# Macaron encoder kernel: second token tiles turned inside the preceding product, eps on VectorE, the last columns in parts, the S5's gated tiles pipelined

## The chip, the cores and the metric

The kernel runs on one core of one Trainium2 chip. The metric is the device time of one execution in microseconds. On the core, TensorE (PE) multiplies, VectorE (DVE), ScalarE (ACT) and GpSimd (POOL) do the elementwise work, and SyncE (SP) issues most of the loads. Each engine executes its own instructions in program order and waits on semaphores for the others.

## The reference

Two layers on a sequence of 256 tokens with 1024 channels, batch 1, fp32. Each layer has three sub-layers, each of which ends in a LayerNorm.

```python
for i in range(DEPTH):                                   # DEPTH = 2
    h = _layernorm(DN_ALPHA * h + 0.5 * _swiglu(h, ffn_w_in[i, 0], ffn_w_out[i, 0]), ln_g[i, 0], ln_b[i, 0])
    mix = _s5_mixer(h, ...) if i % N_MIXERS == 0 else _gmlp_mixer(h, ...)
    h = _layernorm(DN_ALPHA * h + mix, ln_g[i, 1], ln_b[i, 1])
    h = _layernorm(DN_ALPHA * h + 0.5 * _swiglu(h, ffn_w_in[i, 1], ffn_w_out[i, 1]), ln_g[i, 2], ln_b[i, 2])

def _swiglu(x, w_in, w_out):                             # 1024 -> 2 x 2816 -> 1024
    gate, up = jnp.split(x @ w_in, 2, axis=-1)
    return (jax.nn.silu(gate) * up) @ w_out
...
    y = jax.nn.gelu(y)                                   # end of _s5_mixer; y from the scan
    z = y * jax.nn.sigmoid(y @ w_glu + b_glu)
    return z @ w_out
...
    z = jax.nn.gelu(x @ w_in + b_in)                     # start of _gmlp_mixer
    u, v = jnp.split(z, 2, axis=-1)
    v = _layernorm(v, ln_g, ln_b)
```

## The kernel before

**Tiles.** The tokens are two tiles of 128, t = 0 and 1; `h[t]` (128 tokens x 1024 channels) is the running state. A product needs the channels on the partitions, so `make_xt(t)` turns h of a tile: eight PE transposes of 128x128 into two PSUM tiles (`tps`, L187), an ACT cast of each (L192) that gives `xt` hi, and a DVE subtract (L193) that gives `xt` lo. Every fp32 product is made of three (`mm3`: hi by hi, hi by lo, lo by hi; L201, L202, L203, or L208 to L210 for the products that keep the weights in place).

**Weights.** `Stream` ws brings the weights in blocks of 128x2048 in the order of their use: a load by SP into one of three raw buffers, an ACT cast to hi, a DVE subtract to lo, into one of five slots. `ws.tick(n)` splits up to n blocks and issues the loads that have become possible, so where a tick stands in the code sets where the split stands in ACT's and DVE's order (L96, L97).

**Order.** The sub-layers run ffn, s5, ffn, ffn, gmlp, ffn. The code is written in the order that the engines execute (`tc.manual_schedule()`); nothing moves instructions afterwards. An FFN has 11 chunks of 256 hidden columns, and its second product is accumulated chunk by chunk.

**The end of a sub-layer, `close`.** The last products run tile by tile, t = 0 with columns 0 to 511 and 512 to 1023, then t = 1. After each half DVE forms r from h and the PSUM tile (`layernorm_half`, L239) and its statistics (L240), then `layernorm` aggregates them (L247), `rstd_of` makes the reciprocal deviation on POOL in two instructions (eps added, L221; the power -0.5, L222), and `normalize` does r by gamma (L228) and then times rstd plus beta (L231), all in halves of 512. `make_xt(0)` of the next sub-layer stands inside the products of t = 1. In the last sub-layer there is no next one, and each half of h goes out by a DMA, one from SP and one from ACT.

**The start of the next FFN.** Chunks 0 and 1 are made one tile at a time by `step_in(c, t)`, a product of 24 matmuls of 512 (8 slices of k by 3) into the PSUM tile `ips`, then `in_act`: silu on ACT and the gate product on DVE (`sgg`, L358). `step_in(c, 1)` turns the gated tiles of both chunks on PE in its middle (`finish_g`, L348). The order is (0,0), (1,0), `make_xt(1)`, (0,1), (1,1). In the gMLP `step_v` does the same for v (`zps`).

**The end of the S5.** `finish(n)` for eight tiles of 128 channels: DVE makes the gated product (L1164), a cast (DVE for n < 3, L1168; ACT from 3 on, L1170), and a DVE subtract to lo (L1171). z lies in two buffers in turn. Two halves of a weight block's subtract (`rest(1)`, L119) stand after n = 1 and n = 3. The output product of the S5 follows (`close_mixer`).

Of the kernel before, what the change touches and what calls it, by code (L numbers as in the profile page):

```python
# [154 lines left out]
def hybrid(ctx: ExitStack, tc: tile.TileContext, a: dict, out: bass.AP, subs=SUBS):  # L155
# [63 lines left out]
    def rstd_of(mv, eps):  # L219
        rstd = st_p.tile([P, 2], F32, tag="rstd", name="rstd")  # L220
        nc.gpsimd.tensor_scalar(rstd[:, 0:1], mv[:, 1:2], eps, 1.0, op0=ALU.add, op1=ALU.mult)  # L221
        nc.gpsimd.tensor_tensor(rstd[:, 1:2], rstd[:, 0:1], mhalf, op=ALU.pow)  # L222
        return rstd[:, 1:2]
# [51 lines left out]

    def close(li, si, acc, blocks, mm, gb, hscale, eps, last):

        order = [(n, j) for n in range(2) for j in range(len(blocks))]
        for t in range(2):
            for n, j in order:  # L280
                for kt in range(2):
                    mm(j, t, n, kt, acc[t][n])
                    if (t, n, j, kt) == (1, 1, len(blocks) - 2, 0) and not last:
# [12 lines left out]
            if last:
                for n in range(2):
                    s = slice(512 * n, 512 * n + 512)
                    (nc.sync, nc.scalar)[n].dma_start(out=out[0, P * t:P * t + P, s], in_=h[t][:, s])
# [33 lines left out]
    def ffn(ids, li, si, first, last):  # L333
# [146 lines left out]
        close(li, si, acc, [ids["out"][c] for c in range(c0, NCH)], lambda j, t, n, kt, ps: mm_out(c0 + j, t, n, kt, ps),  # L480
# [48 lines left out]
    def gmlp(plan, par, pool, li, si, first, last):  # L529
# [61 lines left out]
        pend = [step_v(0, 0), step_v(1, 0)]  # L591
        make_xt(1)
# [426 lines left out]
    def s5(plan, res, qp, li, si, first, last):  # L1019
# [140 lines left out]
        def finish(n):  # L1160

            x = half(n)
            z = buf["o"][n % 2][:, 0].rearrange("p q k -> p (q k)")
# [7 lines left out]
            V.tensor_tensor(yx(n, 1), z, yx(n, 0).bitcast(F32), op=SUB)  # L1171
# [182 lines left out]
```

## Time and profile before

| | |
|---|---|
| time, median of 3 runs | 971.5 us (970.46 to 971.52) |
| profiled execution | 971.83 us, span 969.7 us, mean granted clock 0.998 |
| PE busy | 944.7 us, 97% of the span |
| DVE busy | 650.9 us, 67% |
| ACT busy | 426.5 us, 44% |
| POOL busy | 162.8 us, 17% |
| PE clock, 40 slices | 9 in every slice |
| moved | 195.10 MB, mean 201 GB/s |

Busy shares are averages over stages with different limits. In timeline rows the first number is the start and the second the time covered, both in us, then the engine, the line, the operation, what it writes and reads, its shape and how many instructions the row joins; in brackets stand the idle time before it and what ended that. Neighbouring instructions of one engine overlap a little, so that a row that joins several is shorter than their sum. A row of waits has the total in us, the number of times, and the longest. A row of windows has busy time and instructions (x) of PE, its weight loads (PEld), DVE, ACT and POOL, then the granted clock, the DMA share and GB/s.

### The profile page before, as it was taken

The page shows a single profiled execution, that of the slowest core. Times are in us where ns is not written, and L with a number is a line of the kernel's source. Part 1 is how long each engine was busy: PE and PEld are TensorE (multiplying, and loading weights), DVE is VectorE, ACT ScalarE, POOL GpSimd, SP SyncE. Part 2 cuts the span into 40 slices and gives each one's busy share as a digit, 9 for nine tenths or more (in the row PEclk, how much of TensorE's full clock was granted, in tenths as well). Part 3 has the DMA queues.
Part 4 walks back from the last instruction along what each step waited for, and adds up shares of the span by engine and source line. Part 5 has one row for each costly group of instructions (what it writes and reads, how often), then busy time and mean ns, then how long its engine had stood idle before and what let it go on. Part 6 is the DMA issues. An engine that isn't in the chain of part 4 may idle for free.

```text
span 969.7 us, 16611 instructions
## 1 busy us (share of the span) xinstructions
PE 944.7 (97%) x6988; PEld 857.9 (88%) x6988; DVE 650.9 (67%) x805; ACT 426.5 (44%) x504; POOL 162.8 (17%) x240
## 2 busy tenths in 40 slices
PE   7999999999999999999999999999999999999996
PEld 5999999978896799999987999999889879999995
DVE  5889998787998774554667636455788866453635
ACT  5465347535342553434433534353445444444430
POOL 1888910011750100000001000000011010000001
PEclk9999999999999999999999999999999999999999
DMA  8887796958646566365547765636357468465521
GB/s 276 219 249 228 237 318 203 315 200 300 208 141 220 174 198 236 132 224 167 185 163 239 255 222 166 225 133 227 121 173 261 130 203 268 138 220 172 184 78 43
DMA packets 133898, 195.10 MB, mean 201 GB/s; under 512 B 7632, under 2 KB 104576, under 8 KB 133824
## 3 DMA queue, kind: packets, MB, share of 16 engines
q1 hardware_dynamic: 129152, 182.61, 56.8%
q0 software_dynamic: 4384, 10.92, 3.9%
q8 instruction: 54, 0.88, 0.4%
q10 hardware_dynamic: 288, 0.52, 0.1%
q14 instruction: 20, 0.16, 0.0%
HBM read 184.07 MB, written 9.96 MB: 200 GB/s over the span
## 4 chain that ended last, share of the span: by engine, by line
PE 68%; DVE 8%; ACT 2%; issue 1%; POOL 1%; DMA 1%; POOLq 0%; DVEq 0%; ACTq 0%
PE ips L210 11%; PE ips L209 11%; PE ips L208 11%; PE acc L201 7%; PE acc L202 7%; PE acc L203 7%; DVE lo L97 3%; PE pps L1080 2%; PE ips L203 1%; ACT hi L96 1%; DVE lo L89 1%; DMA raw<-in_s_w_in 1%; PE ips L201 1%; PE ips L202 1%; PE zps L209 1%
## 5 line engine op out<-in xcount | busy, mean ns | idle before, releaser
L210 PE MATMUL ips<-xt,lo 128*128 128x256 f32 x1184 | 335.2, 283 | 2.2 <-DVE lo L89 2.2
L208 PE MATMUL ips<-xt,hi 128*128 128x256 f32 x1184 | 335.4, 283 | 0.0
L209 PE MATMUL ips<-xt,hi 128*128 128x256 f32 x1184 | 335.0, 283 | 0.0
L89 DVE TENSOR_TENSOR lo<-raw,hi 128x2048 fp32r<-128x2048 f32 x107 | 242.9, 2291 | 8.7 <-ACT hi L88 8.3
L210 PEld LDWEIGHTS ips<-xt,lo 128*128 128x128 f32 x1184 | 227.1, 192 | 2.6 <-DVE lo L89 2.6
L208 PEld LDWEIGHTS ips<-xt,hi 128*128 128x128 f32 x1184 | 227.1, 192 | 1.5
L209 PEld LDWEIGHTS ips<-xt,hi 128*128 128x128 f32 x1184 | 227.1, 192 | 1.4
L88 ACT CAST hi<-raw 128x2048 fp32r<-128x2048 f32 x107 | 203.9, 1909 | 46.4 <-PE acc L203 26.6
L398 DVE TENSOR_TENSOR sgg<-ips,sgg 128x256 f32<-128x256 f32 x74 | 31.1, 420 | 166.1 <-ACT sgg L397 166.0
L201 PE MATMUL acc<-hi,gt 128*128 128x512 f32 x352 | 137.9, 392 | 0.2 <-ACT gt L406 0.2
L202 PE MATMUL acc<-lo,gt 128*128 128x512 f32 x352 | 137.4, 390 | 0.0
L203 PE MATMUL acc<-hi,gt 128*128 128x512 f32 x352 | 137.0, 389 | 0.0
L397 ACT ACTIVATE sgg<-ips 128x256 f32<-128x256 f32 x74 | 28.4, 383 | 216.4 <-PE ips L210 213.5
L221 POOL TENSOR_SCALAR rstd<-mv 128x1 f32<-128x1 f32 x14 | 10.4, 741 | 634.6 <-DVE mv L247 610.8
L97 DVE TENSOR_TENSOR lo<-raw,hi 128x2048 fp32r<-128x2048 f32 (+2 forms) x52 | 89.6, 1754 | 22.7 <-ACT hi L96 22.6
L203 PEld LDWEIGHTS acc<-hi,gt 128*128 128x128 f32 x352 | 66.1, 188 | 14.3 <-DVE gt L407 0.2
L201 PEld LDWEIGHTS acc<-hi,gt 128*128 128x128 f32 x352 | 66.2, 188 | 13.2 <-ACT gt L406 0.6
L202 PEld LDWEIGHTS acc<-lo,gt 128*128 128x128 f32 x352 | 66.3, 188 | 12.2
L96 ACT CAST hi<-raw 128x2048 fp32r<-128x2048 f32 (+2 forms) x52 | 74.5, 1482 | 4.2 <-DMA raw<-in_ffn_w_in 2.5
L407 DVE TENSOR_TENSOR gt<-sgg,gt 128x256 fp32r<-128x256 f32 x74 | 32.4, 438 | 61.8 <-ACT gt L406 61.8
L406 ACT CAST gt<-sgg 128x256 fp32r<-128x256 f32 x74 | 30.1, 406 | 58.2 <-DVE sgg L398 58.2
L201 PE MATMUL ips<-hi,xt 128*128 128x512 f32 x112 | 46.0, 410 | 3.6 <-ACT xt L192 2.3
(229 smaller groups left out, 1222.1 us busy)
## 6 DMA issues: line engine op xcount, KB each, us to landing
raw<-in_ffn_w_in SPq DMA_DIRECT2D x172, 512.0 KB, 5.7
raw<-in_ffn_w_out SPq DMA_DIRECT2D x44, 1024.0 KB, 5.1
raw<-in_g_w_in SPq DMA_DIRECT2D x8, 1024.0 KB, 6.0
rows<-w SPq DMA_DIRECT2D x8, 512.0 KB, 6.3
raw<-in_s_w_in SPq DMA_DIRECT2D x4, 1024.0 KB, 8.4
raw<-in_s_w_glu SPq DMA_DIRECT2D x4, 1024.0 KB, 5.0
w<-rows SPq DMA_DIRECT2D x8, 512.0 KB, 5.8
tc<-tc SPq DMA_DIRECT2D x16, 256.0 KB, 5.5
```

The source lines that it names most:

```text
L88: nc.scalar.copy(hi, raw)
L89: self.unfinished.append(lambda: nc.vector.tensor_tensor(lo, raw, hi.bitcast(F32), op=ALU.subtract))
L96: nc.scalar.copy(hi[:, s], raw[:, s])
L97: eng[p % len(eng)].tensor_tensor(lo[:, s], raw[:, s], hi[:, s].bitcast(F32), op=ALU.subtract)
L201: nc.tensor.matmul(ps, xh, wh, start=start, stop=False)
L202: nc.tensor.matmul(ps, xh, wl, start=False, stop=False)
L203: nc.tensor.matmul(ps, xl, wh, start=False, stop=stop)
L208: nc.tensor.matmul(ps, wh, xh, start=start, stop=False)
L209: nc.tensor.matmul(ps, wh, xl, start=False, stop=False)
L210: nc.tensor.matmul(ps, wl, xh, start=False, stop=stop)
L398: nc.vector.tensor_tensor(g, ps[:, 1], sg, op=ALU.mult)
L407: nc.vector.tensor_tensor(x[:, 1], g, x[:, 0].bitcast(F32), op=ALU.subtract)
```

## The change

It has four parts. (1) `rstd_of` adds eps on DVE; the power stays on POOL. (2) In the last sub-layer `close_last` takes the place of `close`: columns 512 to 1023 of t = 1 are finished as two products 256 wide in PSUM tiles of their own (`ops`), after the partial sum of the earlier chunks has gone into r; the statistics of t = 1 are taken in 256s, and its output leaves in three DMAs (512, 256, 256). (3) `step_in(1, 0)` and `step_v(1, 0)` take `make_xt(1)` into their middle, after five of the eight slices of k; `step_in(0, 0)` and `step_v(0, 0)` split no block, and step (1, 0) splits its block right behind `make_xt(1)`. (4) `finish(n)` returns the subtract, which is issued after `finish(n + 1)`; z lies in four buffers, tiles 3 and 5 subtract on POOL, and the two halves of the weight block's subtract stand after n = 4 and n = 5.

```diff
     def rstd_of(mv, eps):
         rstd = st_p.tile([P, 2], F32, tag="rstd", name="rstd")
-        nc.gpsimd.tensor_scalar(rstd[:, 0:1], mv[:, 1:2], eps, 1.0, op0=ALU.add, op1=ALU.mult)
+        nc.vector.tensor_scalar(rstd[:, 0:1], mv[:, 1:2], eps, 1.0, op0=ALU.add, op1=ALU.mult)
         nc.gpsimd.tensor_tensor(rstd[:, 1:2], rstd[:, 0:1], mhalf, op=ALU.pow)
...
+    def close_last(acc, blocks, mm, gb, hscale, eps):
+        for t in range(2):
+            r = ln_p.tile([P, D], F32, tag="r", name="r", bufs=2)
+            parts = [(0, 512), (512, 512)] if t == 0 else [(0, 512), (512, 256), (768, 256)]
+            step = parts[-1][1]
+            st = st_p.tile([P, D // step, 6], F32, tag="bst", name="bst")
+            if t == 1:
+                s = slice(512, D)
+                nc.vector.scalar_tensor_tensor(r[:, s], in0=h[t][:, s], scalar=hscale, in1=acc[t][1], op0=ALU.mult, op1=ALU.add)
+            for i, (c, w) in enumerate(parts):
+                s, n = slice(c, c + w), c // 512
+                ps = acc[t][n] if w == 512 else mm_p.tile([P, 512], F32, tag="mm", name="ops")[:, 0:w]
+                for j in range(len(blocks)):
+                    for kt in range(2):
+                        mm(j, t, n, kt, ps, (c % 512, w), w < 512 and j == 0 and kt == 0)
...
+                x, scale = (h[t], hscale) if w == 512 else (r, 1.0)
+                nc.vector.scalar_tensor_tensor(r[:, s], in0=x[:, s], scalar=scale, in1=ps, op0=ALU.mult, op1=ALU.add)
+                for x in range(c, c + w, step):
+                    nc.vector.bn_stats(st[:, x // step], r[:, x:x + step])
+            mv = st_p.tile([P, 2], F32, tag="mv", name="mv")
+            nc.vector.bn_aggr(mv, st)
+            rstd, (g, b) = rstd_of(mv, eps), gb
...
+            for i, (c, w) in enumerate(parts):
+                s = slice(c, c + w)
+                nc.vector.scalar_tensor_tensor(h[t][:, s], in0=r[:, s], scalar=rstd, in1=b[:, s], op0=ALU.mult, op1=ALU.add)
+                (nc.sync, nc.scalar)[i % 2].dma_start(out=out[0, P * t:P * t + P, s], in_=h[t][:, s])
...
-        def step_in(c, t):
+        def step_in(c, t, mid=None, split=1):
             ps = mm_p.tile([P, 512], F32, tag="mm", name="ips")
-            in_mm(ids["in"][c], t, ps, range(4))
+            cut = 5 if mid else 4
+            in_mm(ids["in"][c], t, ps, range(cut))
+            if mid:
+                mid()
             if t:
                 finish_g()
-            ws.tick()
-            in_mm(ids["in"][c], t, ps, range(4, KD))
+            ws.tick(split)
+            in_mm(ids["in"][c], t, ps, range(cut, KD))
             in_act(c, t, ps)
             if t == 1:
                 done(ids["in"][c])
-            ws.tick()
+            ws.tick(split)
...
-            step_in(0, 0)
-            step_in(1, 0)
-            make_xt(1)
+            step_in(0, 0, split=0)
+            step_in(1, 0, lambda: make_xt(1))
             step_in(0, 1)
             step_in(1, 1)
...
-        pend = [step_v(0, 0), step_v(1, 0)]
-        make_xt(1)
+        pend = [step_v(0, 0, split=0), step_v(1, 0, lambda: make_xt(1))]
...
         def finish(n):
             x = half(n)
-            z = buf["o"][n % 2][:, 0].rearrange("p q k -> p (q k)")
+            z = buf["o"][n % 2][:, n // 2 % 2].rearrange("p q k -> p (q k)")
...
-            V.tensor_tensor(yx(n, 1), z, yx(n, 0).bitcast(F32), op=SUB)
+            return lambda: (G if n in (3, 5) else V).tensor_tensor(yx(n, 1), z, yx(n, 0).bitcast(F32), op=SUB)
...
+        second = lambda: None
         for n in range(CT):
-            finish(n)
-            if n in (1, 3):
+            x = finish(n)
+            second()
+            second = x
+            if n in (4, 5):
                 rest(1)
+        second()
```

In the listings below a name carries the number of its tile: h0 and h1 are h of the two token tiles, ips the product of a step, tps a transposed tile in PSUM, sgg a gated tile, lo82 and hi82 the weight block with number 82. Each instruction stands with its line in that kernel.

PE where FFN 2 of layer 0 meets FFN 1 of layer 1, before: the end of step (1, 0), the transposes, the start of step (0, 1).

```order
L203 MATMUL ips_5478<-hi81_5415,xt_96 128x512
L187 MATMUL tps_5506<-ident_85,h1_95 128x128 x4
L187 MATMUL tps_5513<-ident_85,h1_95 128x128 x4
L201 MATMUL ips_5520<-hi78_5274,xt_96 128x512
L202 MATMUL ips_5520<-lo78_5275,xt_96 128x512
L203 MATMUL ips_5520<-hi78_5274,xt_96 128x512
```

PE at the same place after:

```order
L201 MATMUL ips_5471<-hi81_5415,xt_96 128x512
L202 MATMUL ips_5471<-lo81_5416,xt_96 128x512
L203 MATMUL ips_5471<-hi81_5415,xt_96 128x512
L187 MATMUL tps_5487<-ident_85,h1_95 128x128 x4
L187 MATMUL tps_5494<-ident_85,h1_95 128x128 x4
L201 MATMUL ips_5471<-hi81_5415,xt_96 128x512
L202 MATMUL ips_5471<-lo81_5416,xt_96 128x512
L203 MATMUL ips_5471<-hi81_5415,xt_96 128x512
```

The transposes of h1 stand nine matmuls of step (1, 0) earlier, and those nine follow them.

DVE at that place, before: the split of blocks 81 and 82, the gate products of chunks 0 and 1, the lo parts of xt.

```order
L97 TENSOR_TENSOR lo81_5416<-raw81_5282,hi81_5415 128x512 x4
L97 TENSOR_TENSOR lo82_5457<-raw82_5295,hi82_5456 128x2048
L358 TENSOR_TENSOR sgg_5475<-ips_5443,sgg_5475 128x256
L358 TENSOR_TENSOR sgg_5503<-ips_5478,sgg_5503 128x256
L193 TENSOR_TENSOR xt_96<-tps_5506,xt_96 128x512
L193 TENSOR_TENSOR xt_96<-tps_5513,xt_96 128x512
L352 TENSOR_TENSOR gt_5536<-tps_5533,gt_5536 128x128
```

DVE there after:

```order
L97 TENSOR_TENSOR lo81_5416<-raw81_5282,hi81_5415 128x512 x4
L392 TENSOR_TENSOR sgg_5468<-ips_5443,sgg_5468 128x256
L193 TENSOR_TENSOR xt_96<-tps_5487,xt_96 128x512
L193 TENSOR_TENSOR xt_96<-tps_5494,xt_96 128x512
L97 TENSOR_TENSOR lo82_5502<-raw82_5295,hi82_5501 128x2048
L392 TENSOR_TENSOR sgg_5517<-ips_5471,sgg_5517 128x256
L386 TENSOR_TENSOR gt_5536<-tps_5533,gt_5536 128x128
```

The subtract of block 82 moved from ahead of the gate products to behind the two of xt, and the gate product of chunk 1 stands behind it. ACT's cast of block 82 moved in the same way, behind its two casts of xt and ahead of the silu of chunk 1.

DVE at the end of the S5, before, the first four of the eight tiles (rot is z or the gate, y the scan's output, lo44 the weight block whose subtract is done in halves):

```order
L1164 SCALAR_TENSOR_TENSOR rot_2668<-rot_2664,y_2517 128x4x64
L1168 CAST xt_96<-rot_2668 128x2x128
L1171 TENSOR_TENSOR xt_96<-rot_2668,xt_96 128x2x128
L1164 SCALAR_TENSOR_TENSOR rot_2669<-rot_2664,y_2517 128x4x64
L1168 CAST xt_96<-rot_2669 128x2x128
L1171 TENSOR_TENSOR xt_96<-rot_2669,xt_96 128x2x128
L119 TENSOR_TENSOR lo44_3490<-raw44_3321,hi44_3489 128x1024
L1164 SCALAR_TENSOR_TENSOR rot_2668<-rot_2665,y_2517 128x4x64
L1168 CAST xt_96<-rot_2668 128x2x128
L1171 TENSOR_TENSOR xt_96<-rot_2668,xt_96 128x2x128
L1164 SCALAR_TENSOR_TENSOR rot_2669<-rot_2665,y_2517 128x4x64
L1171 TENSOR_TENSOR xt_96<-rot_2669,xt_96 128x2x128
```

DVE there after:

```order
L1203 SCALAR_TENSOR_TENSOR rot_2668<-rot_2664,y_2517 128x4x64
L1207 CAST xt_96<-rot_2668 128x2x128
L1203 SCALAR_TENSOR_TENSOR rot_2669<-rot_2664,y_2517 128x4x64
L1207 CAST xt_96<-rot_2669 128x2x128
L1210 TENSOR_TENSOR xt_96<-rot_2668,xt_96 128x2x128
L1203 SCALAR_TENSOR_TENSOR rot_2668<-rot_2665,y_2517 128x4x64
L1207 CAST xt_96<-rot_2668 128x2x128
L1210 TENSOR_TENSOR xt_96<-rot_2669,xt_96 128x2x128
L1203 SCALAR_TENSOR_TENSOR rot_2669<-rot_2665,y_2517 128x4x64
L1210 TENSOR_TENSOR xt_96<-rot_2668,xt_96 128x2x128
L1203 SCALAR_TENSOR_TENSOR rot_2668<-rot_2666,y_2518 128x4x64
L119 TENSOR_TENSOR lo44_3490<-raw44_3321,hi44_3489 128x1024
```

A tile's subtract stands behind the next tile's product (and cast), the subtract of tile 3 is gone from DVE, and the halves of lo44 stand later. On POOL the subtracts of tiles 3 and 5 stand ahead of the DMAs that load gamma and beta of that sub-layer's LayerNorm.

More of the change, by code (lines that the diff above doesn't have):

```diff
@@ L274, in new_acc @@
         return [acc_p.tile([P, 512], F32, tag="acc", name="acc") for _ in range(2)]
+    def close_last(acc, blocks, mm, gb, hscale, eps):
[13 more added lines that the diff above has]
+                        mm(j, t, n, kt, ps, (c % 512, w), w < 512 and j == 0 and kt == 0)
+                    if t == 0 and i == 0 and j < 2:
+                        ws.tick()
+                    if (t, i) == (1, len(parts) - 1):
+                        ws.done(blocks[j])
+                x, scale = (h[t], hscale) if w == 512 else (r, 1.0)
[5 more added lines that the diff above has]
+            rstd, (g, b) = rstd_of(mv, eps), gb
+            for n in range(2):
+                s = slice(512 * n, 512 * n + 512)
+                nc.vector.scalar_tensor_tensor(r[:, s], in0=r[:, s], scalar=mv[:, 0:1], in1=g[:, s], op0=ALU.subtract, op1=ALU.mult)
+            for i, (c, w) in enumerate(parts):
+                s = slice(c, c + w)
+                nc.vector.scalar_tensor_tensor(h[t][:, s], in0=r[:, s], scalar=rstd, in1=b[:, s], op0=ALU.mult, op1=ALU.add)
+                (nc.sync, nc.scalar)[i % 2].dma_start(out=out[0, P * t:P * t + P, s], in_=h[t][:, s])
@@ L276, in close @@
     def close(li, si, acc, blocks, mm, gb, hscale, eps, last):
+        if last:
+            return close_last(acc, blocks, mm, gb, hscale, eps)
         order = [(n, j) for n in range(2) for j in range(len(blocks))]
@@ L282, in close @@
                     mm(j, t, n, kt, acc[t][n])
-                    if (t, n, j, kt) == (1, 1, len(blocks) - 2, 0) and not last:
+                    if (t, n, j, kt) == (1, 1, len(blocks) - 2, 0):
                         make_xt(0, next_kind[li, si] == "s5")
@@ L290, in close @@
                     sums = layernorm_half(t, acc[t][0], 0, hscale)
-            if t == 1 and not last:
+            if t == 1:
                 ws.tick(1)
             layernorm(t, acc[t], gb, hscale, eps, sums)
-            if t == 1 and not last and next_kind[li, si] != "s5":
+            if t == 1 and next_kind[li, si] != "s5":
                 ws.tick(1, 4)
[L296 to L299, printed above, removed]
     def plan_ffn(li, fi, fine):
@@ L439, in start_in, with mm_out @@
             done(ids["in"][0])
-        def mm_out(c, t, n, kt, ps):
+        def mm_out(c, t, n, kt, ps, cols=(0, 512), start=False):
             gh, gl = (gts[c, kt][:, j, P * t:P * t + P] for j in range(2))
             wh, wl = ws.get(ids["out"][c])
-            s = slice(D * kt + 512 * n, D * kt + 512 * n + 512)
-            mm3(ps, gh, gl, wh[:, s], wl[:, s], c == 0 and kt == 0, c == NCH - 1 and kt == 1)
+            s = slice(D * kt + 512 * n + cols[0], D * kt + 512 * n + sum(cols))
+            end = NCH - 4 if last and (t, n) == (1, 1) and cols[1] == 512 else NCH - 1
+            mm3(ps, gh, gl, wh[:, s], wl[:, s], start or c == 0 and kt == 0, c == end and kt == 1)
         def step_out(c, t):
@@ L479, in ffn @@
         c0 = NCH - 3
-        close(li, si, acc, [ids["out"][c] for c in range(c0, NCH)], lambda j, t, n, kt, ps: mm_out(c0 + j, t, n, kt, ps),
+        close(li, si, acc, [ids["out"][c] for c in range(c0, NCH)], lambda j, *args: mm_out(c0 + j, *args),
               gb, 2 * ALPHA, 4 * EPS, last)
```

13 lines of the change are left out of this document (8 added, 5 removed).

## The prediction

> **What bounds the kernel now.** I read first the engine totals (the table ahead), then the list of what TensorE (PE) waited for, then windows between the joints of the sub-layers, then the timeline engine by engine at each place where a wait stood.
>
> ```profile
> PE tps L187 <- DVE h L231: 2.3, 2, 1.5
> PE ips L201 <- ACT xt L192: 2.3, 3, 0.8
> PE acc L201 <- ACT xt L1170: 1.5, 3, 0.5
> 341.00:505.00 164.00, 164.00 (x1132) 153.46 (x1131) 88.28 (x81) 67.48 (x70) 1.69 (x2) 1.00 0.58 193
> ```
>
> Inside an FFN PE never stops: from 341 to 505 it was busy 164.00 of 164.00 us, at a granted clock of 1.00. The number of matmuls is almost the same after the change, so time can only come from the waits. The three waits shown (us in total, times, longest) are 6.1 us, and they stand where the change works: LayerNorm's result (h) before its transposes, the second token tile's operand (xt) at the three entries of an FFN, and the gated tiles at the S5's end; the gMLP's entry is shown below. A wait also costs the interval in which PE starts again, so each loss below is taken from start to start.
>
> **The joints (step_in, step_v).** Here FFN 2 of layer 0 meets FFN 1 of layer 1.
>
> ```profile
> 505.19 1.03 PE L187 MATMUL tps<-ident,h 128*128 128x128 f32 x8
> 506.76 0.39 PE L201 MATMUL acc<-hi,gt 128*128 128x512 f32 x1
> 510.68 1.92 ACT L96 CAST hi<-raw 128x2048 fp32r<-128x2048 f32 x1
> 515.83 4.69 DVE L97 TENSOR_TENSOR lo<-raw,hi 128x512 fp32r<-128x512 f32 x5
> 519.22 1.03 PE L187 MATMUL tps<-ident,h 128*128 128x128 f32 x8
> 519.86 1.07 ACT L192 CAST xt<-tps 128x512 fp32r<-128x512 f32 x2
> 520.44 0.75 DVE L358 TENSOR_TENSOR sgg<-ips,sgg 128x256 f32<-128x256 f32 x2
> 521.11 1.28 DVE L193 TENSOR_TENSOR xt<-tps,xt 128x512 fp32r<-128x512 f32 x2
> 522.18 0.39 PE L201 MATMUL ips<-hi,xt 128*128 128x512 f32 x1
> 524.25 0.60 PE L348 MATMUL tps<-ident,sgg 128*128 128x128 f32 x4
> 709.96 1.03 PE L187 MATMUL tps<-ident,h 128*128 128x128 f32 x8
> 712.76 0.40 PE L201 MATMUL zps<-hi,xt 128*128 128x512 f32 x1
> ```
>
> Tile 0's eight transposes are followed by products that don't need them: from 505.19 to the fourth matmul behind them, 506.76, it is 1.57 us. Tile 1's are followed by their own users: 519.22 to 522.18 is 2.96 us for the same count. The joint loses 2.96 - 1.57 = 1.39 us. The wait list's "2.3, 3, 0.8" says that the three FFN entries are alike, so they lose 4.17. The gMLP's, 709.96 to 712.76, loses 2.80 - 1.57 = 1.23. Together 5.40.
>
> After the change the transposes stand nine matmuls earlier, 9 x 0.23 = 2.07 us (522.18 to 524.25 is nine intervals of 0.23). Call their start T0. PE has those nine to do while ACT casts: the casts began 0.64 after T0 and take 1.07, so they are done at T0 + 1.71, and PE's first use comes at T0 + (1.57 - 3 x 0.23) + 2.07 = T0 + 2.95. DVE's two subtracts (1.28) end by T0 + 2.4, since the block's 2048-wide subtract no longer stands ahead of them. That stall is gone. Is h of tile 1 there? It was complete at 515.9, where DVE's next work (515.83) begins, and the transposes now come at 519.22 - 2.07 = 517.15: 1.2 us to spare.
>
> What is late next: the moved split. ACT's cast of 2048 (1.92) follows the casts, T0 + 1.6 to 3.5; DVE's subtract follows it. Of the five subtracts from 515.83 to 520.52 the four 512-wide make a quarter of 2.3 each, so the big one takes 2.3: T0 + 3.55 to 5.85. Behind it stands the gate product of chunk 1 (two take 0.75): T0 + 6.2. PE reaches that tile's transposes at T0 + 2.95 + 12 x 0.23 + 0.22 = T0 + 5.92 (0.22 for the two transposes of chunk 0 ahead of them, a quarter of eight). So PE waits 0.3 and starts again, 0.35 at three FFN entries, 1.05. In the gMLP the additions to v stand there and PE does not read them for a while: 0. The load of the next raw block is issued about 2.5 us later, and the block that the moved split reads was already cast at 510.68, eight microseconds before its new place, so no transfer gets onto the path. **Joints: 5.40 - 1.05 = 4.35; bounds 2.5 (0.6 more at each of the three entries) and 4.9.**
>
> **eps on VectorE.**
>
> ```profile
> 962.78 0.21 DVE L247 BATCH_NORM_AGGREGATE mv<-bst 128x2 f32<-128x12 f32 x1
> 963.03 1.42 DVE L228 SCALAR_TENSOR_TENSOR r<-r,mv,gam 128x512 f32<-128x512 f32 x2
> 963.08 0.75 POOL L221 TENSOR_SCALAR rstd<-mv 128x1 f32<-128x1 f32 x1 [6.38 <-DVE mv L247]
> 963.91 0.94 POOL L222 TENSOR_TENSOR rstd<-rstd,mhalf 128x1 f32<-128x1 f32 x1
> 964.89 1.41 DVE L231 SCALAR_TENSOR_TENSOR h<-r,rstd,bet 128x512 f32<-128x512 f32 x2 [0.44 <-POOL rstd L222]
> L645 DVE TENSOR_SCALAR ch<-ch 128x32 f32<-128x32 f32 x3 | 0.6, 197 | 0.1
> ```
>
> POOL takes 0.75 for eps and 0.94 for the power, and DVE idles 0.44 before it can apply rstd. On DVE the same operation is nearest to the 128x32 row, 0.197. It lets POOL end 0.5 earlier and delays L228 by about 0.1, so h begins as soon as L228 is through: 0.35 earlier (bounds 0, if the small instruction costs as much as POOL's, and 0.45, the whole idle time). There are 14 such LayerNorms. It counts where PE waits for h: at the S5's entry (the 1.5 of the wait list's first row) it is all on the path, **0.35**; at the S5's end and in the tail it is inside those sums; elsewhere PE has other products to run (341 to 505 and the joints above) and it is worth nothing.
>
> **The S5's end.**
>
> ```profile
> 289.96 0.63 DVE L1164 SCALAR_TENSOR_TENSOR rot<-rot,y 128x256 f32<-128x256 f32 x1 [0.52 <-ACT rot L1158]
> 290.63 0.29 DVE L1168 CAST xt<-rot 128x256 fp32r<-128x256 f32 x1
> 297.21 0.39 PE L201 MATMUL acc<-hi,xt 128*128 128x512 f32 x1
> 303.14 0.42 DVE L1171 TENSOR_TENSOR xt<-rot,xt 128x256 fp32r<-128x256 f32 x1 [0.53 <-ACT xt L1170]
> 303.73 0.39 PE L203 MATMUL acc<-hi,xt 128*128 128x512 f32 x1
> 304.95 4.49 DVE L97 TENSOR_TENSOR lo<-raw,hi 128x2048 fp32r<-128x2048 f32 x2 [1.39 <-ACT hi L96]
> 309.36 0.68 DVE L239 SCALAR_TENSOR_TENSOR r<-h,acc 128x512 f32<-128x512 f32 x1
> 313.97 0.39 PE L203 MATMUL acc<-hi,xt 128*128 128x512 f32 x1
> 315.14 1.29 PE L187 MATMUL tps<-ident,h 128*128 128x128 f32 x8 [0.78 <-DVE h L231]
> 283.35 2.89 DVE L119 TENSOR_TENSOR lo<-raw,hi 128x1024 fp32r<-128x1024 f32 x2
> 292.62 1.22 DVE L119 TENSOR_TENSOR lo<-raw,hi 128x1024 fp32r<-128x1024 f32 x1
> 283.72 1.43 POOL L1132 TENSOR_TENSOR xt<-y,xt 128x256 fp32r<-128x256 f32 x1 [3.81 <-ACT xt L1125]
> 287.60 0.76 POOL L1132 TENSOR_TENSOR xt<-y,xt 128x256 fp32r<-128x256 f32 x1 [2.45 <-ACT xt L1125]
> bet<-in_ln_b POOLq DMA_DIRECT2D x1, 512.0 KB, 7.2
> ```
>
> From 297.21 to 303.73 PE starts 17 intervals in 6.52 us; at 0.23 they are 3.9. It waits there for tiles 5, 6 and 7 one after the other, because each goes DVE product, ACT cast, DVE subtract, with DVE idle (0.53) in between. That is 2.62 lost. After the change DVE does the next product in that gap. Replaying its new order with these durations, the first two subtracts come later by a product (0.63), less 0.1 since neighbours that do not depend on each other overlap: PE +0.53. Eight products of 0.6, three casts of 0.3, six subtracts of 0.35 (the overlap taken off) and two halves of a lo block of 1.15 are 10.1 us from 289.96, so tile 7's subtract ends at 300.1 instead of 303.56; PE wants it at 297.21 + 0.53 + 3.9 = 301.65. The stretch loses nothing more: 2.62 - 0.53 = 2.1.
>
> ACT, too, is through with the tiles some 3.7 us earlier, so DVE's two lo blocks behind them move by as much, end at 305.7, and the LayerNorm begins there instead of at 309.36. Its first half of h was ready at 315.0, 5.7 later; now at 305.65 + 5.7 - 0.35 (eps) = 311.0, while PE comes to the transposes at 314.2 - 2.1 = 312.1. The wait before 315.14 goes too: 313.97 to 315.14 is 0.94 over its 0.23, and the eight transposes take 1.29 there against 1.03 at 505.19; I take 1.1 together. POOL has sub 3 and sub 5 (0.76 to 1.43 each) ahead of the two loads for gamma and beta, which will be issued at about 298; the later took 7.2 to land, and L228 wants gamma at about 308.5 and L231 beta at 310, so some 3 us remain. **S5's end: 2.1 + 1.1 = 3.2; bounds 1.5 and 3.6.**
>
> The unknown is DVE beside POOL. Two 1024-wide subtracts took 2.89 together while POOL subtracted, against 1.22 each alone: 0.45 lost by DVE, and POOL 1.43 instead of 0.76. Twice 0.45 puts tile 7 at 301.0 and h at 311.9, which leaves 0.65 and 0.2, so I take nothing off. [...] The rows show both engines giving way in part, so I stay with them.
>
> **The last columns (close_last).**
>
> ```profile
> 961.33 0.69 DVE L239 SCALAR_TENSOR_TENSOR r<-h,acc 128x512 f32<-128x512 f32 x1 [1.85 <-PE acc L203]
> 962.05 0.69 DVE L240 BATCH_NORM_STATS2 bst<-r 128x6 f32<-128x512 f32 x1
> out<-h ACTq DMA_DIRECT2D x2, 256.0 KB, 2.1
> 350.00:354.00 4.00, 4.00 (x36) 4.00 (x35) 3.45 (x5) 0.89 (x4) 0.00 (x0) 1.00 1.02 358
> ```
>
> The last 18 matmuls of 512 become 36 of 256. The window 350 to 354 holds only 256-wide ones, 36 in 4 us, 0.11 each: 36 x 0.11 to 0.12 against 18 x 0.23 is -0.1 to +0.2; I take +0.1. Behind them r and its statistics are half as wide: 0.69 + 0.69 become 0.42 each (the gate product is as wide), -0.55, and rstd is 0.35 earlier. h is written in three pieces, as many columns as in two before. The early sum into r and the extra statistics have DVE idle 1.85 to hide in. The output lands 2.1 after its issue; the last is now half as big and a third shares the queues: 0. **Tail: 0.55 + 0.35 - 0.1 = 0.8; bounds 0** (three outputs landing later, 256-wide products slower than inside the FFN) **and 1.0.**
>
> **Sum.** 0.35 + 4.35 + 3.2 + 0.8 = 8.7 us off the profiled execution's own 971.83: 963.1. The median shown, 971.5, lies 0.33 below that execution, so the prediction is 962.8.
>
> **The rivals.** (a) The joint's wait moves instead of shrinking: the moved split takes longer beside the nine matmuls, and the gate product is 0.6 later still at three entries, or h of tile 1 misses its earlier transposes. For it: the replay leaves PE 0.3 short already, there is no cover. Price 4.35 - 2.5 = 1.85, 964.6. (b) DVE and POOL block each other at the S5's end, and h stays late there: 0.75 to 1.7 of 3.2 lost. For it the 2.89 and 1.43 rows, in which both lost; against it that 0.45 twice still fits. It gives 963.5 to 964.5. (c) Slower: the moved split's raw block has not landed when ACT, which works in order, comes to it; then the gate's activation, the product and PE stand behind it with no cover. It must be late at all three FFN entries by (8.7 + 1.9) / 3 = 3.5 us for the kernel to be slower by 0.2%, about 973.5. Against it: that block was in at 510.68 and its new place is about 518.7. (d) Nothing changes, 971: the waits on PE only shift to the next instruction in every part. Against it: between the joints PE has no other wait.
>
> **How the numbers follow.** A measurement of this kernel can tell about 0.2%, 1.9 us, from no change. The forecast, 961.3 to 964, has 0.60; (a) 0.17; (b) 0.13; both together, 965 to 967.5, 0.04; (d) 0.03; (c) 0.03. Faster 0.94, same 0.03, slower 0.03. Summing the lower bounds of all four parts (0 + 2.5 + 1.5 + 0) gives 4.0 and 967.5, the upper (0.45 + 4.9 + 3.6 + 1.0) 9.95 and 961.5, both less 0.33 already; I take 961.2 to 966.8.
>
> **What would show it.** In the waits of the changed kernel, xt before L201 and before zps should be gone, and a short wait of the gate's transposes on DVE's product should be new, 0.3 three times. The eighteen matmuls of the S5's last six tiles should start within 3.9 us. The S5's last h should not be waited for. At the S5's entry PE's wait of 1.5 should read about 1.2. The last output should be issued 0.7 sooner after PE's last matmul. The prediction is wrong if L201 still waits for xt, if DVE's 1024-wide subtracts at the S5's end are well over 1.7, or if PE has a new wait inside an FFN.

## Result and the profile after

The changed kernel takes 962.44 us (median; 961.81 to 963.75), the kernel before beside it 971.51; the ratio is 0.9897, 95% interval 0.9875 to 0.992. The forecast was 962.8. The profiled execution took 962.43 us with a span of 960.6, against 971.83 and 969.7.

The list of what PE waited for in the changed kernel (us in total, times, longest), from where it touches the change:

```profile
PE tps L382 <- DVE sgg L392: 0.6, 3, 0.2
...
PE acc L203 <- DVE xt L1210: 0.4, 2, 0.2
PE tps L187 <- DVE h L231: 0.3, 1, 0.3
```

The window inside an FFN, as before from 341 on:

```profile
341.00:495.00 154.00, 154.00 (x1079) 144.83 (x1078) 80.69 (x70) 64.41 (x66) 0.00 (x0) 1.00 0.58 191
```

The waits of L201 and zps for xt are gone; three short waits of the gate's transposes (L382) on DVE's product are new, and so are two at the start of the S5's output product (L203 for a tile's lo part). The wait for h fell from 2.3 to 0.3. Inside an FFN PE stays at 154.00 of 154.00.

At the S5's entry the shorter wait is not all time gained, as the transposes of h show, first before, then after:

```profile
206.72 1.23 PE L187 MATMUL tps<-ident,h 128*128 128x128 f32 x8 [1.53 <-DVE h L231]
206.15 1.23 PE L187 MATMUL tps<-ident,h 128*128 128x128 f32 x8 [0.30 <-DVE h L231]
```

They start 0.57 earlier; the other 0.66 of the 1.23 is PE coming there later (205.85 instead of 205.19).

Where the time came from is read best from the starts of PE's transposes of token tile 0, which the change did not move against PE's other work (starts in us, differences worked out):

| | before | after | ahead by | gained in the stretch |
|---|---|---|---|---|
| S5's entry, L187 | 206.72 | 206.15 | 0.57 | 0.57 |
| S5's end, L187 | 315.14 | 311.86 | 3.28 | 2.71 |
| FFN to FFN, L187 | 505.19 | 500.51 | 4.68 | 1.40 |
| FFN to gMLP, L187 | 695.95 | 690.05 | 5.90 | 1.22 |
| gMLP to FFN, L187 | 769.30 | 762.00 | 7.30 | 1.40 |
| first of the last columns' matmuls | 957.05 | 948.59 | 8.46 | 1.16 |
| last output issued | 966.33 | 957.27 | 9.06 | 0.60 |

The joint between two FFNs, after, PE, ACT and DVE:

```profile
512.28 1.04 PE L187 MATMUL tps<-ident,h 128*128 128x128 f32 x8
512.92 1.07 ACT L192 CAST xt<-tps 128x512 fp32r<-128x512 f32 x2 [3.40 <-PE tps L187]
513.54 1.29 DVE L193 TENSOR_TENSOR xt<-tps,xt 128x512 fp32r<-128x512 f32 x2
513.88 1.93 ACT L96 CAST hi<-raw 128x2048 fp32r<-128x2048 f32 x1
515.85 2.29 DVE L97 TENSOR_TENSOR lo<-raw,hi 128x2048 fp32r<-128x2048 f32 x1 [1.02 <-ACT hi L96]
517.95 0.38 PE L382 MATMUL tps<-ident,sgg 128*128 128x128 f32 x2
518.05 0.42 DVE L392 TENSOR_TENSOR sgg<-ips,sgg 128x256 f32<-128x256 f32 x1
518.53 0.44 PE L382 MATMUL tps<-ident,sgg 128*128 128x128 f32 x2 [0.20 <-DVE sgg L392]
```

The gate product ends 6.19 us after the transposes' start (518.47 - 512.28; the replay had 6.2), and PE, which reached it at 518.17, goes on at 518.53: 0.36 lost, three times.

### The profile page after: what moved, and what is told of

Same layout as the page of the kernel before. It is cut to its first block, busy times and chain, and to the rows that moved or that the text cites. A ratio compares the mean times of both kernels' runs of the same rounds, so it can differ in the third digit from the quotient of the medians.

```text
span 960.6 us, 16654 instructions
## 1 busy us (share of the span) xinstructions
PE 942.0 (98%) x7006; PEld 859.7 (89%) x7006; DVE 651.4 (68%) x822; ACT 426.4 (44%) x504; POOL 154.3 (16%) x228
## 4 chain that ended last, share of the span: by engine, by line
PE 75%; DVE 2%; ACT 1%; POOL 0%; issue 0%; DVEq 0%; POOLq 0%; ACTq 0%
PE ips L210 11%; PE ips L209 11%; PE ips L208 11%; PE acc L203 8%; PE acc L201 8%; PE acc L202 8%; PE ips L203 2%; PE ips L201 2%; PE ips L202 2%; PE pps L1119 2%; PE tps L187 1%; PE zps L210 1%; PE zps L209 1%; PE zps L208 1%; PE ups L203 1%; PE ups L201 1%
## 5 line engine op out<-in xcount | busy, mean ns | idle before, releaser
L201 PE MATMUL acc<-hi,gt 128*128 128x512 f32 x346 | 135.6, 392 | 0.5 <-ACT gt L443 0.5
L202 PE MATMUL acc<-lo,gt 128*128 128x512 f32 x346 | 135.1, 390 | 0.0
L203 PE MATMUL acc<-hi,gt 128*128 128x512 f32 x346 | 134.7, 389 | 0.0
L222 POOL TENSOR_TENSOR rstd<-rstd,mhalf 128x1 f32<-128x1 f32 x14 | 13.3, 951 | 628.1 <-DVE rstd L221 628.1
L203 PEld LDWEIGHTS acc<-hi,gt 128*128 128x128 f32 x346 | 65.0, 188 | 14.0 <-DVE gt L444 0.3
L201 PEld LDWEIGHTS acc<-hi,gt 128*128 128x128 f32 x346 | 65.1, 188 | 13.7 <-ACT gt L443 1.3
L201 PE MATMUL ips<-hi,xt 128*128 128x512 f32 x112 | 45.9, 410 | 1.1 <-ACT hi L106 1.1
```

The source lines that it names most:

```text
L201: nc.tensor.matmul(ps, xh, wh, start=start, stop=False)
L202: nc.tensor.matmul(ps, xh, wl, start=False, stop=False)
L203: nc.tensor.matmul(ps, xl, wh, start=False, stop=stop)
```

## Experiments

The kernel before took 972.63 to 972.86 us beside these runs, and the ratios are against that. The 962.44 of the changed kernel was not measured again beside them. Runs of one kernel differ by 1.5 to 7 us, so a difference of a microsecond between two medians says little; where the text decides between theories, it does so by the stretches of each kernel's one profiled execution.

**The joints alone**, on the kernel before.

```diff
...
-            step_in(0, 0)
-            step_in(1, 0)
-            make_xt(1)
+            step_in(0, 0, split=0)
+            step_in(1, 0, lambda: make_xt(1))
...
```

> The kernel before with the joints alone changed (make_xt(1) after five slices in the middle of step (1, 0) and of step_v(1, 0), no split in step (0, 0)). Theory A: the waits of xt go, 1.39 + 1.39 + 1.39 + 1.23, and a wait of the gate's transposes of 0.36 comes at three FFN entries; the fifth slice's wait (about 0.17 each, owed to eps) stays. 4.3 us, 967.2. Theory B: the whole shift that the two traces show at the joints, 5.2 us, belongs to this part: 966.3, and the fifth slice's product no longer waits.

968.07 us, ratio 0.9946 (0.9928 to 0.9964). From one row of L187 to the next, at equal work, the four joints gained 1.08, 1.09, 1.19 and 1.01, together 4.37. Theory A. The gate's transposes wait as foreseen, and DVE's piece for the fifth slice still holds PE up a little.

Its waits (the 3.8 is at the S5's entry and is taken up below):

```profile
PE tps L187 <- DVE h L231: 4.6, 2, 3.8
...
PE tps L348 <- DVE sgg L358: 0.5, 3, 0.2
```

In its timeline of the first joint the third matmul of the fifth slice starts 0.33 after the second instead of 0.23; at the other three joints the two intervals of that slice are 0.16 to 0.17 too long together:

```profile
329.73 0.39 PE L201 MATMUL ips<-hi,xt 128*128 128x512 f32 x1
329.96 0.50 PE L202 MATMUL ips<-lo,xt 128*128 128x512 f32 x1
330.29 0.39 PE L203 MATMUL ips<-hi,xt 128*128 128x512 f32 x1
```

**The S5's end alone**, on the kernel before: `finish` and its loop as in the change.

> The kernel before with the S5's end alone changed (subtracts one tile later, z in four buffers, tiles 3 and 5 on POOL, the halves of the lo block after tiles 4 and 5). Theory A: 2.1 us in the output product, and h of tile 0 comes 3.2 earlier on DVE against PE's 2.1, so that the wait before its transposes (0.94) shrinks to nothing or a few tenths without eps: 3.0 to 3.2, about 968.4. Theory B (the output product's gain is eaten by the wait for h, since the two lo blocks and the LayerNorm behind them set the end): h moves by less than 2.5 and the kernel gains 2.5 or less, 969.0 or more.

969.63 us, ratio 0.9968 (0.995 to 0.9985). From the last transposes ahead of the S5's loop to those behind it (L187 of tile 1, 220.86, to L187 of tile 0, 314.99) it is 94.13 us, before 97.10: 2.97 gained, theory A. PE hardly waited for h there even without eps on VectorE: the transposes start 0.28 after the last product instead of 0.23 and lose 0.2 in their middle, where they need the second half of h.

**eps back on POOL**, in the changed kernel.

```diff
-        nc.vector.tensor_scalar(rstd[:, 0:1], mv[:, 1:2], eps, 1.0, op0=ALU.add, op1=ALU.mult)
+        nc.gpsimd.tensor_scalar(rstd[:, 0:1], mv[:, 1:2], eps, 1.0, op0=ALU.add, op1=ALU.mult)
```

> The changed kernel with eps back on POOL; the other three parts stay. Theory A (the trace after the change: from the aggregate to h it is 1.64 us instead of 2.12 at the S5's entry): eps is worth 0.48 at the S5's entry, 0.42 in the tail, and also some 0.17 at each of the four joints, because h of tile 1 and with it the four 512-wide lo pieces of DVE come earlier and the fifth slice's product no longer waits for its piece (0.10 and more over 0.23 before the change). 1.5 us in all: about 964.0, and the L202 wait of the fifth slice is back in step (1, 0). Theory B (the prediction's): it counts only at the S5's entry and in the tail, 0.35 each, 963.1, with no wait in step (1, 0).

965.36 us, ratio 0.9918 (0.9888 to 0.9947): 2.9 more than the changed kernel. The profiled span is 3.9 longer, in these pieces: 0.42 from the second weight block's cast to the transposes of h at the S5's entry (9.94 against 9.52); 0.73 since that block's cast began later; 1.5 in a slow stretch of PE behind it; 0.43, 0.18, 0.16 and 0.17 between the transposes of tile 0 and those of tile 1 at the four joints; 0.5 in the tail; less 0.25 in the S5's scan loop; that and the slow stretch are taken up below. So theory A holds for the places it names, and misses these two.

**eps alone**, on the kernel before (the same line the other way).

> The kernel before with eps on VectorE as the only change. Theory A (from putting it back on POOL in the changed kernel: 0.50 from the aggregate to h at the S5's entry, 0.17 at each of the four joints where the fifth slice waits for its lo piece, 0.49 in the tail): in the kernel before also 0.5 at the S5's end, where PE waits for h: 2.1 us, about 969.4, apart from what the clock does behind the S5's entry. Theory B (the prediction's): 0.35 at the S5's entry, 0.35 at the S5's end, 0.35 in the tail: 1.05, 970.4.

969.10 us, ratio 0.9967 (0.9946 to 0.9987); its profiled span is 966.5, 3.1 less. By stretches that is 0.90 at the S5's entry (0.78 of it because the second weight block's cast began at 196.00 instead of 196.78), 0.16 at the S5's end, 0.45, 0.53, 0.16 and 0.45 at the joints and 0.48 in the tail. At the S5's end the wait for h shrinks by the 0.5 of theory A (0.78 to 0.31), but PE loses 0.31 in the scan loop ahead of it. And beside the places of theory A eps shortens the old waits for xt themselves, from 2.3 to 1.4 in total at the three FFN joints, because DVE's whole row there is earlier. Part of what eps brings is therefore what the joints bring too: the four parts do not add up.

Its group of eps instructions (busy us, mean ns of one, idle before):

```profile
L221 DVE TENSOR_SCALAR rstd<-mv 128x1 f32<-128x1 f32 x14 | 2.1, 154 | 0.5
```

**The last columns undone**, in the changed kernel: two parts of 512, no early sum.

```diff
-            parts = [(0, 512), (512, 512)] if t == 0 else [(0, 512), (512, 256), (768, 256)]
+            parts = [(0, 512), (512, 512)]
...
```

> The changed kernel with the last columns of tile 1 again as one product of 512 (no early sum into r, statistics in 512s, two output DMAs); eps stays on VectorE. Theory A: from the trace, PE's last 36 matmuls cost 0.23 more until DVE can start, r and statistics save 0.53 and the third piece of h costs 0.12, so the parts are worth 0.2 and the rest of the tail's gain is eps: 962.6. Theory B (the prediction's): the parts alone are worth 0.45: 962.9. The time can hardly tell the two apart; the tail's rows, from PE's last matmul to the last output's issue, can (5.42 before the change, 4.49 after; A: 4.9 to 5.0).

963.36 us, ratio 0.9898 (0.9871 to 0.9926). From PE's last matmul (952.62) to the last output's issue (957.57) 4.95 us: theory A. Counted from the first matmul of these columns, the issue comes 8.80 us later, 8.68 in the changed kernel and 9.28 before, so the parts are worth 0.12 and eps 0.48.

**The transposes after seven slices**, in the changed kernel (the same line in `step_in` and in `step_v`).

```diff
-            cut = 5 if mid else 4
+            cut = 7 if mid else 4
```

> The changed kernel with make_xt(1) after seven of the eight slices instead of five: three matmuls behind the transposes instead of nine. Theory A (what hides the casts is the products behind the transposes, 0.23 each): PE's first use of xt comes 0.88 + 0.69 = 1.57 after the transposes' start, ACT's first cast ends at 1.22 and DVE's first subtract at about 1.9 after it, so only the third matmul waits, 0.1 to 0.3; at the same time the gate's transposes come 1.38 earlier against the split that moves with the transposes, no change there. About 963. Theory B: it does not matter where in the product the transposes stand, as long as something is behind them: 962.4, with no wait on xt.

968.06 us, ratio 0.9955 (0.9939 to 0.997): both theories wrong. The list has no wait for xt at the FFN entries (at the gMLP's 0.3), but the gate's transposes lose 1.6 each from start to start. The list of waits:

```profile
PE tps L382 <- DVE sgg L392: 4.3, 3, 1.5
```

And the timeline of the first of them:

```profile
325.38 1.04 PE L187 MATMUL tps<-ident,h 128*128 128x128 f32 x8
...
328.93 2.29 DVE L97 TENSOR_TENSOR lo<-raw,hi 128x2048 fp32r<-128x2048 f32 x1 [1.01 <-ACT hi L96]
331.14 0.42 DVE L392 TENSOR_TENSOR sgg<-ips,sgg 128x256 f32<-128x256 f32 x1
```

The chain behind the transposes is again 6.2 us (331.56 - 325.38), but PE has 1.38 us less to do until it needs its end. My expectation said that this would cancel, and had the sign of it wrong: the split moves with the transposes, PE's need of the gate product does not.

**After four slices**, in the same two places.

```diff
-            cut = 5 if mid else 4
+            cut = 4
```

> The changed kernel with make_xt(1) after four of the eight slices instead of five: twelve matmuls behind the transposes. Theory A (the chain cast, split, gate product behind the transposes takes 6.2 us whatever PE does, so each matmul behind them is 0.23 of cover until the chain is covered, as after seven slices each one less cost 0.2): the gate's wait of 0.36 goes at three entries, and h of tile 1 is still there (1.2 to spare, 0.69 used): 1.1 less, 961.3. Theory B (the gate product waits for something that does not move with the transposes, ACT's silu of the whole step): the wait stays, 962.4.

961.63 us, ratio 0.9884 (0.9864 to 0.9904). The gate's wait is gone: in the timeline the product ends (329.91) before PE arrives.

```profile
323.73 1.03 PE L187 MATMUL tps<-ident,h 128*128 128x128 f32 x8
329.49 0.42 DVE L392 TENSOR_TENSOR sgg<-ips,sgg 128x256 f32<-128x256 f32 x1
330.07 0.60 PE L382 MATMUL tps<-ident,sgg 128*128 128x128 f32 x4
```

The stretches from one L187 to the next are 0.42, 0.40, 0.00 (gMLP) and 0.45 shorter, 1.3 in all. Against that the S5's entry came 0.76 later in this execution, after a later load, so its time shows less. Theory A.

**The split behind the gate product**, in the changed kernel with the five slices.

```diff
-            ws.tick(split)
+            ws.tick(0 if mid else split)
             in_mm(ids["in"][c], t, ps, range(cut, KD))
...
```

> The changed kernel with the moved split once more later: in step (1, 0) and step_v(1, 0) it stands behind the gate product (behind the whole step), not behind make_xt(1). Theory A: the gate's transposes wait 0.36 at three FFN entries because DVE's gate product stands behind the 2048-wide subtract; with the product first that wait goes and the block has time until chunk 2: 1.1 us less, 961.3. Theory B: the wait moves on, to the gated tiles' casts and subtracts, which now stand behind the block on ACT and DVE: no gain, 962.4, with a new PE wait in step (0, 1) or (1, 1).

960.93 us, ratio 0.9876 (0.9851 to 0.9902), theory A. The same stretches are again 0.42, 0.40, 0.00 and 0.45 shorter, the wait of L382 is out of the list, and no wait takes its place: DVE does the product first (327.11) and the block after it, as its timeline shows.

```profile
327.11 0.42 DVE L392 TENSOR_TENSOR sgg<-ips,sgg 128x256 f32<-128x256 f32 x1 [1.01 <-ACT sgg L391]
328.91 2.29 DVE L97 TENSOR_TENSOR lo<-raw,hi 128x2048 fp32r<-128x2048 f32 x1 [1.37 <-ACT hi L96]
329.22 0.60 PE L382 MATMUL tps<-ident,sgg 128*128 128x128 f32 x4
```

**All subtracts of the S5's end on DVE**, in the changed kernel.

```diff
-            return lambda: (G if n in (3, 5) else V).tensor_tensor(yx(n, 1), z, yx(n, 0).bitcast(F32), op=SUB)
+            return lambda: V.tensor_tensor(yx(n, 1), z, yx(n, 0).bitcast(F32), op=SUB)
```

> The changed kernel with the subtracts of tiles 3 and 5 on DVE instead of POOL. Theory A (DVE and POOL block each other): DVE's products beside POOL's subtracts took 1.15 and about 1.0 instead of 0.62, so DVE loses 0.95 to spare itself two subtracts of 0.34; back on DVE its row is 0.3 shorter in all, and since PE has slack there the time stays, 962.4. Theory B (POOL takes real work off DVE): DVE's row is 0.7 longer, and h of tile 0 comes 0.7 later; PE has some 0.2 to 0.5 of slack there and the time grows by 0.2 to 0.5.

961.92 us, ratio 0.9888 (0.9862 to 0.9915), no difference that these runs can tell, and the S5's stretch from L187 to L187 is as long as in the changed kernel, 105.72 us against 105.71. DVE needs 10.23 us from its first product to its last subtract (290.39 to 300.62), 10.63 with two subtracts on POOL (289.71 to 300.34). The rows of the changed kernel show why:

```profile
294.19 1.86 POOL L1210 TENSOR_TENSOR xt<-rot,xt 128x256 fp32r<-128x256 f32 x1 [6.08 <-issue]
294.23 1.22 DVE L119 TENSOR_TENSOR lo<-raw,hi 128x1024 fp32r<-128x1024 f32 x1
295.37 1.15 DVE L1203 SCALAR_TENSOR_TENSOR rot<-rot,y 128x256 f32<-128x256 f32 x1
297.09 1.41 POOL L1210 TENSOR_TENSOR xt<-rot,xt 128x256 fp32r<-128x256 f32 x1 [1.05 <-ACT xt L1209]
297.83 1.61 DVE L1203 SCALAR_TENSOR_TENSOR rot<-rot,y 128x256 f32<-128x256 f32 x2
```

POOL's subtract starts at 294.19 and takes 1.86, while DVE's block subtract beside it runs at its usual 1.22; then DVE's product takes 1.15 instead of 0.62. The second pair is alike (1.41, and the first of the two products takes 1.15). Both times POOL is through 0.6 after DVE's block subtract (296.05 after 295.45, 298.50 after 297.90). In the scan loop of the same execution four subtracts of this shape took POOL 0.73 (L1171), 1.1 and 0.7 less. With all subtracts on DVE the products behind its block subtracts take 0.62 and 0.60. Theory A: both engines take longer where POOL subtracts beside DVE, DVE by about 0.5 in its next instruction for each subtract of POOL, and PE has the slack.

**The LayerNorm ahead of the late weight block**, in the kernel with the split behind the gate product.

```diff
-                if t == 0 and n == 0 and j < 2:
+                if t == 0 and n == 0 and j < (0 if next_kind[li, si] == "s5" else 2):
                     ws.tick()
...
             layernorm(t, acc[t], gb, hscale, eps, sums)
+            if t == 0 and next_kind[li, si] == "s5":
+                ws.tick()
```

> The kernel with the split behind the gate product, and in addition the second weight block of the S5 is split (cast and subtract) behind the LayerNorm of token tile 0 instead of ahead of it. In the runs so far that block's load landed between 196.6 and 198.0 us, and h of tile 0 followed the cast by 9.44 (eps on VectorE) or 9.94 (eps on POOL) every time, so PE waited 0.3 to 3.8 us; where it waited 1.89 or more, the granted clock was 0.5 for some 3 to 4 us behind it. Theory A (DVE's order makes the LayerNorm wait for the load, and the wait makes the slow clock): h is ready some 2 us before PE, no wait, no slow stretch, 959.7, and the runs spread less. Theory B (the block itself is late for the S5's first product, the order does not matter): the wait moves from h to that product, 960.9.

960.37 us (959.08 to 961.02), ratio 0.9872 (0.9851 to 0.9892): the fastest of all, though its interval covers the kernel without this step. The trace is clear where the times are not. The block came late in this execution, and PE did not notice:

```profile
198.08 1.91 ACT L96 CAST hi<-raw 128x2048 fp32r<-128x2048 f32 x1 [3.10 <-DMA raw<-in_s_w_in]
201.62 1.41 DVE L231 SCALAR_TENSOR_TENSOR h<-r,rstd,bet 128x512 f32<-128x512 f32 x2
202.94 2.29 DVE L97 TENSOR_TENSOR lo<-raw,hi 128x2048 fp32r<-128x2048 f32 x1
204.36 1.03 PE L187 MATMUL tps<-ident,h 128*128 128x128 f32 x8
```

With the old order the transposes would have come at 198.08 + 9.44 = 207.5 (an estimate from the 9.44 of the other executions). Theory A for the wait and the slow stretch: the matmuls behind the transposes start 0.23 apart (205.69, 205.92). The four runs still spread over 1.9 us, as did those of the changed kernel (in the kernel without this step it was 3.1), so something else moves them too. That is open.

## Why the prediction was right, and where it was off

**The joints (4.35 forecast).** Right in mechanism and size: 4.37 with this part alone, and the new wait of the gate's transposes is 0.36 three times where 0.35 was forecast. The stretches of the changed kernel show 5.18, and the difference, some 0.8, belongs to eps and, with 0.26, to the transposes at the S5's end, which run in 1.03 instead of 1.29.

**eps on VectorE.** The step that failed is that "elsewhere PE has other products to run" and eps "is worth nothing" there. The earlier h of tile 1 lets DVE begin the next block's four lo pieces earlier (by 0.48 at the joint of the two layers, counted from the transposes of tile 0), and PE's fifth slice no longer waits for its piece: with eps back on POOL 0.18, 0.16 and 0.17 are lost again at three joints, and 0.43 at the first, of which 0.26 is the transposes' restart that the prediction had in its S5 part. I had seen PE free of waits from 341 to 505 and called the joints covered too. The sizes were low as well: the instruction took 0.154, not 0.197, and PE's transposes of h followed the cast by 9.44 instead of 9.94, so eps is worth 0.50 at the S5's entry and 0.48 in the tail, where 0.35 was forecast and 0.45 was the upper bound.

**The S5's end (3.2 forecast).** 2.97 alone. The eighteen matmuls of the last six tiles start within 3.85 us, 3.9 was forecast; the changed kernel's timeline:

```profile
297.57 0.39 PE L201 MATMUL acc<-hi,xt 128*128 128x512 f32 x1
301.42 0.39 PE L203 MATMUL acc<-hi,xt 128*128 128x512 f32 x1
306.14 0.68 DVE L239 SCALAR_TENSOR_TENSOR r<-h,acc 128x512 f32<-128x512 f32 x1
311.86 1.03 PE L187 MATMUL tps<-ident,h 128*128 128x128 f32 x8
```

The wait for h is gone (311.86 carries none). The changed kernel shows 2.71 in this stretch because PE lost 0.31 at 242.9 in the scan loop, where the kernel before lost nothing. That is a cost of eps on VectorE: the loss stands in all eight profiled executions with it, eps alone among them, and in none of the four with eps on POOL. PE waits there for a sum that POOL makes; POOL begins these sums 24.27 to 24.29 after tile 1's transposes in the eight and 23.96 to 23.98 in the four. Why POOL begins later is not shown. The list of DMA issues has beta's landing (KB each, us from issue to landing):

```profile
bet<-in_ln_b POOLq DMA_DIRECT2D x1, 512.0 KB, 8.7
```

It was issued at 299.0, so it was there 2.8 ahead of its use at 310.5, as forecast.

**The last columns (0.8 forecast).** 0.60 measured to the last issue. What failed is the term of 0.1 for PE's products, and two costs that were put at nothing. The halves of r and the statistics take 0.42 and 0.43 and save 0.53, as forecast. But the last of the 36 matmuls starts 4.19 after the first, where the last of the 18 started 3.86 after its first (957.05 to 960.91); DVE begins 0.32 behind it instead of 0.43, so the products cost 0.2, not 0.1. The aggregate takes 0.26 instead of 0.21, and the third piece of h costs 0.12. The column parts are worth 0.12 instead of 0.45, and the rest of the tail, 0.48, is eps. The timeline of the last columns, after:

```profile
948.59 0.28 PE L201 MATMUL ops<-hi,gt 128*128 128x256 f32 x1
952.78 0.28 PE L203 MATMUL ops<-hi,gt 128*128 128x256 f32 x1
953.10 0.42 DVE L298 SCALAR_TENSOR_TENSOR r<-r,ops 128x256 f32<-128x256 f32 x1 [1.13 <-PE ops L203]
953.55 0.43 DVE L300 BATCH_NORM_STATS2 bst<-r 128x6 f32<-128x256 f32 x1
954.02 0.26 DVE L302 BATCH_NORM_AGGREGATE mv<-bst 128x2 f32<-128x24 f32 x1
955.71 1.53 DVE L309 SCALAR_TENSOR_TENSOR h<-r,rstd,bet 128x512 f32<-128x512 f32 x3
```

35 intervals in 4.19 us are 0.12 each; the 0.11 that I read from a window of busy PE, by counting what began or ended in it, was too low.

**The rivals.** (a) did not come, since the chain behind the transposes was 6.2 as replayed, but the run with seven slices shows how near it was: with six matmuls of cover less the gate's wait grew by 1.25, 0.2 for each. (b) came and cost no time: POOL's subtracts took 1.86 and 1.41, DVE's product behind each 1.15 instead of 0.62, so DVE lost about 0.5 each time. No run shows the 0.75 to 1.7 that (b) was priced at: with POOL's two subtracts and without them the S5's stretch is 105.71 and 105.72. In all four places POOL is through 0.6 after DVE's subtract beside it, the two of the prediction's rows included (285.16 after 284.56, 288.37 after 287.76), and DVE's next instruction is 0.53 or 0.54 late. So the rows do not show both engines giving way in part, as the prediction read them: the first of its two DVE subtracts took its usual 1.22 and the second 1.76. (c) and (d) did not come: no block was late at a joint, and the only wait that moved on is the gate's, as forecast.

**The signs.** L201 and zps no longer wait for xt, and PE has no new wait inside the FFN shown. The last output is issued 0.94 sooner after PE's last matmul (4.49 instead of 5.43) where 0.7 was forecast, since that matmul itself comes later. PE's wait at the S5's entry reads 0.30 where 1.2 was forecast, because PE came there later. And one sign watched the wrong instruction: DVE's 1024-wide subtracts took 1.22 and 1.20, far from the 1.7 that would have told of rival (b), while the loss fell on the products behind them.

**The total.** It came within 0.4 us, and that is partly luck, because errors cancelled: eps brought about 1 more than forecast at the joints, the S5's entry and the tail, while the column parts (0.33) and the scan loop (0.31) took some 0.65 of it back. The runs of one kernel also spread more than that (961.81 to 963.75).

## What to carry to other kernels

When work is moved so that something else hides it, replay the whole chain behind it up to the next thing the busy engine needs, not only to the first use: here the product that hid the casts had to hide the split and the gate product too, and putting the split behind the gate product, or the transposes one slice earlier, bought another 1.3 us. An instruction that waits for a load belongs behind everything on its engine that does not need the load: with the split behind the LayerNorm PE had no wait at the S5's entry, in an execution where that block's cast began at 198.08, the latest of all. A saving in a chain that is hidden at one place is worth looking up at every other place where the same chain ends in a wait.

## What the runs showed of the hardware

At the S5's entry three waits of PE cost more than their own length. Two kernels there; the windows show PE's busy time and instructions first, and the granted clock as the third number from the end. First the kernel before, where PE had been idle for 1.53 ahead of the transposes at 206.72:

```profile
203.00:207.00 4.00, 2.47 (x13) 1.80 (x12) 3.46 (x6) 0.00 (x0) 1.71 (x2) 1.00 0.61 248
207.00:209.00 2.00, 2.00 (x14) 1.61 (x13) 1.97 (x4) 1.60 (x3) 0.00 (x0) 1.00 0.00 0
209.00:211.00 2.00, 2.00 (x10) 1.64 (x9) 1.34 (x3) 1.38 (x1) 0.00 (x0) 1.00 0.00 0
```

Then the changed kernel with eps on POOL, idle for 1.89 ahead of 207.30:

```profile
203.00:207.00 4.00, 2.41 (x11) 1.67 (x9) 3.43 (x6) 0.00 (x0) 1.71 (x2) 1.00 0.59 242
207.00:209.00 2.00, 1.70 (x9) 1.55 (x10) 1.97 (x4) 0.59 (x1) 0.00 (x0) 0.69 0.00 0
209.00:211.00 2.00, 2.00 (x6) 1.52 (x6) 1.33 (x3) 1.98 (x2) 0.00 (x0) 0.50 0.00 0
211.00:213.00 2.00, 2.00 (x10) 1.67 (x9) 1.56 (x1) 0.40 (x1) 0.00 (x0) 0.96 0.00 0
```

After this idle time of 1.89 the granted clock is 0.69, 0.50 and 0.96 in the three windows from 207 to 213, and between 209.63 and 210.91 the 512-wide matmuls start 0.43 apart instead of 0.23. From these transposes to tile 1's it is 12.83 us (207.30 to 220.13) instead of 11.32 (206.72 to 218.04), so 1.5 was lost on top of the wait. The joints alone (idle 3.82) and the S5's end alone (2.72) show the same, with 2.4 and 1.6 on top; the executions with 1.53 and less do not. Worked out from the clocks of such windows, the half clock lasted about 3.4 us in the first, 6.8 in the joints alone (0.89, 0.50, 0.50, 0.51 from 203 to 213) and 3.4 in the S5's end alone (0.51 and 0.64 from 209 to 213); these are estimates. In the S5's end alone the loss did not follow at once: PE went on at 207.96, and the clock was 1.00 from 207 to 209. How long an idle time it takes for the clock to fall, and what sets when it falls and returns, is not shown; no execution was idle for a time between 1.53 and 1.89 at this place.

The start of the transposes of h at the S5's entry followed the landing of the S5's second weight block. ACT was idle until it for 1.02 in the kernel before, 0.21 in the changed kernel and 2.94 in the joints alone, and its cast began between 196.61 and 198.08 in eleven of the twelve profiled executions (196.00 in eps alone), though the code ahead of it differs in little. With the LayerNorm behind that block the transposes of h followed the cast by 9.94 wherever eps was on POOL (four executions). With eps on VectorE they followed by 9.44 in four, and by 9.52, 9.76 and 9.83 in three in which DVE was still busy with an earlier block's subtract when the cast was done. The changed kernel's 0.57 at this place is 0.42 of that and a block that came 0.15 earlier.
